# Position-bias bands for an attention kernel: laid out by the host, with the last bucket's value taken off on GpSimd, instead of built and spread on the chip

## The chip, the cores and the metric

The kernel runs on one core of a Trainium2 chip. A core has five engines with queues of their own: TensorE (PE; its weight loads are shown as PEld), VectorE (DVE), ScalarE (ACT), GpSimd (POOL) and SyncE (SP), which here only issues DMAs. Sixteen DMA engines move data between DRAM and the on-chip memory. The metric is the device time of one launch in microseconds; lower is better.

## The reference, cut to what matters

One layer of a decoder is computed for a prompt of 512 tokens and for 8 sample sequences of one new token each, which have 1024 past tokens in paged caches. Two mixers run side by side on the same modulated input: a sparse attention of 8 heads with three branches (compressed blocks, selected blocks, sliding window), and a block-sparse attention of another 8 heads (MoBA). Gates, projections and a layer norm follow. Every attention logit gets a bias that depends on the distance between query and key alone, through a table of 32 buckets by 16 heads:

```python
def t5_bucket(dist):
    n = jnp.maximum(dist, 0)
    nf = jnp.maximum(n, 1).astype(jnp.float32)
    large = MAX_EXACT + (jnp.log(nf / MAX_EXACT) / math.log(MAX_DISTANCE / MAX_EXACT)
                         * (N_BUCKETS - MAX_EXACT)).astype(jnp.int32)
    return jnp.where(n < MAX_EXACT, n, jnp.minimum(large, N_BUCKETS - 1))

s_w = jnp.einsum('bqgrd,bkgd->bqgrk', qc, kw) * scale + bias_w      # bias_w from tab[t5_bucket(distance)]
p_w = masked_softmax(s_w, valid_w)
```

From a distance of 128 (MAX_DISTANCE) on, all keys have the last bucket. A softmax doesn't change when one value is added to all its logits. So the kernel works with the bias less that of the last bucket: it is zero for every key that is far enough away, and only a band of 256 keys, those of the query's own block of 128 and the block before it, needs anything added.

## The kernel before, in words

All the work is matrix products on TensorE with float32 values split into a high and a low part (`hl`, `kd` and `q2`, `qx`): a product is three matmuls, and each weight tile is split by ScalarE (L310) and by VectorE or GpSimd (L231). The instructions are written as generators that are merged by their shares of the work (`merge`). From the program the tile framework makes one fixed order for each engine's queue, with semaphores; an engine runs its queue in order. A tile waits for its slot until the tile that had the memory before is no longer read.

The stages are: the adaLN modulation and the first projections (0 to about 50 us in the profile), the other projections with the compression (`phi`, to about 170 us), then eight steps `attend(pi)` of a pair of heads each, merged with the decode for the sample (`dec_a`, `dec_b`) and with further projections, and from about 500 us the gates, the up and output projections and the norm.

The bands go this way. `tables` (L458) multiplies the bucket table (`tabx`) by a matrix that holds, for 384 distances, which bucket is taken and the last one to subtract (L465), and copies the 16 by 384 result to the tile `bs`. Much later, in `phis` (L933), behind the last compression pair, GpSimd issues one DMA that writes each of the 16 rows 128 times to DRAM (`band_d`, L939), with rows 385 apart, 3 MB in all. In the attention, `prepare(pi)` (L956) loads for a pair of heads a tile of 128 x 2 x 256 (`bt`, tag `band`, two slots; L960), with a step of 384 between partitions, so that each query row finds its band shifted by one. `prepare(0)` is called before the first step, `prepare(pi + 1)` at the start of `attend(pi)`. `score` (L1000) adds the band to the logits of the last 256 keys on VectorE (L1011).

`prepare` also makes the split queries: `q2` by ScalarE and VectorE (L968, L969), `qx` by ScalarE and GpSimd (L970, L971). GpSimd also scales the exponentials (`p`, L1017).

SyncE's queue around the first band holds, in this order: a store of key/value rows (L572), the loads of the first two bands (L960), 64 loads of pages for the decode's selected keys (`raw<-slck`, L721), the window keys (L1134) and a bias table for them (`ew`, L1190 and L1191). At the start it holds small loads of constants (L540 to L547) behind those of the modulation weights.

Of the kernel before, what the change touches and what calls it, by code (L numbers as in the profile page):

```python
# [24 lines left out]
BIG = 1e30  # L25
# [26 lines left out]
NORM_N = 512  # L52
LIM_N = 384
PARTS = [512], [512], [512], [256, 256]
BAND_AT = 3
SELI_K = 6
W_FIRST = 3
COPY_ENG = "daa"
# [132 lines left out]
def build(tc, A):  # L191
# [44 lines left out]
    with ExitStack() as es:  # L236
# [25 lines left out]
        def p_e():  # L262
            return bank("e", 1)
# [109 lines left out]
        snew = per.tile([128, 3], F32, name="snew")  # L373
        dn = per.tile([128, 16], F32, name="dn")
        ocmp = per.tile([128, 128], F32, name="ocmp")
        m_d = dram.tile([8, 128, 2, NT], F32, name="m_d")
        band_d = dram.tile([16, 128, 385], F32, name="band_d")
        y = yp.tile([128, 8, NT], F32, name="y", tag="y")

        def const(name, rows=128):  # L380
# [77 lines left out]
        def tables():  # L458

            nc.gpsimd.memset(bc[:, :, 0:16], 0.0)  # L460
            nc.gpsimd.memset(bc[:, :, 31:64], BIG)
            nc.gpsimd.memset(cv2, 0.0)
            nc.gpsimd.memset(zn, 0.0)
            p = p_e()
            mm(p[:16, :384], tabx[:, 0:16], e[:, E_BAND:E_CMP], True, True)  # L465
            bs = st.tile([16, 384], F32, name="bs")
            nc.vector.tensor_copy(bs, p[:16, :384])
            D["band"] = bs
            p = p_e()
            for m in range(15):  # L470
                mm(p[:, m * 8:m * 8 + 8], e[:, E_CMP + m * 128:E_CMP + m * 128 + 128], tabx[:, 0:8], True, True)
            nc.vector.tensor_copy(bc[:, :, 16:31], p[:, :120].rearrange("p (m h) -> p h m", h=8))
            p = p_e()
            mm(p[:, :194], tabx[:, 16:144], e[:, E_DEC:E_WIN], True, True)
            mm(p[:, 256:386], tabx[:, 144:272], e[:, E_DEC:E_DEC + 130], True, True)
            nc.vector.tensor_copy(bdn, p[:, :194])
            nc.vector.tensor_copy(bdm, p[:, 256:386])
# [60 lines left out]
                    early_mm(n, j - 1)  # L538
        with tc.issue_after(ss["dma"].ins):
            nc.sync.dma_start(cstd, A["cst"][:, NC0:NC2])  # L540
            nc.sync.dma_start(pt16, A["pt16"])
            nc.vector.tensor_scalar(vidx, pt16, 16.0, const("p16"), op0=OP.mult, op1=OP.add)
            nc.sync.dma_start(phib, A["phib"])
            nc.sync.dma_start(pos, A["pos"].rearrange("p (a b c) -> p a b c", a=2, b=8))
            nc.sync.dma_start(ptt, A["pt"])
            nc.sync.dma_start(w2, A["w2"])
            nc.sync.dma_start(b2v, bass.AP(tensor=A["b2v"].tensor, offset=A["b2v"].offset, ap=[[0, 128], [1, 64]]))  # L547
# [385 lines left out]
        def phis():  # L933
            yield from phi_prompt(*kcvc)
            for bp in range(4):
                yield from phi_pair(bp)
                if bp == BAND_AT:
                    with tc.issue_after(D["last"].ins):
                        nc.gpsimd.dma_start(band_d[:, :, 0:384], D["band"].unsqueeze(1).to_broadcast([16, 128, 384]))  # L939

        merge(Flow(fills(FILLS[0]), fill_cost(FILLS[0])), Flow(phis(), PHIS))
        drain(dec_cmp())
# [13 lines left out]
        def prepare(pi):  # L956

            h0, hs = (pi, 4) if pi < 4 else (2 * pi, 1)
            bt = at.tile([128, 2, 256], F32, name="band", bufs=2)
            nc.sync.dma_start(bt, bass.AP(tensor=band_d.tensor, offset=band_d.offset + h0 * 128 * 385 + 127,  # L960
                                          ap=[[384, 128], [hs * 128 * 385, 2], [1, 256]]))
            BAND[pi] = bt
            for g in range(2):
                own, oth = OWN[g], OWN[1 - g]

                q2 = at.tile([128, T], F32R, name="q2", bufs=3)
                qx = at.tile([128, T], F32R, name="qx", bufs=3)
                nc.scalar.copy(q2[own], y[own, pi, :T])  # L968
                nc.vector.tensor_sub(q2[oth], y[own, pi, :T], f32(q2[own]))  # L969
                nc.scalar.copy(qx[oth], y[own, pi, :T])  # L970
                nc.gpsimd.tensor_sub(qx[own], y[own, pi, :T], f32(q2[own]))  # L971
                Q2[pi, g] = q2, qx
# [618 lines left out]
def _prepare(inp):  # L1591

    f = lambda a: np.ascontiguousarray(np.asarray(a))
    inp = {k: np.asarray(v) for k, v in inp.items()}
    cst, e = _constants()
    d = {"cst": cst, "e": e}
    call = np.concatenate([inp["c_prompt"], inp["c_sample"]], 0)
    d["cT"] = f(call.T.reshape(8, 128, 9).transpose(1, 0, 2))
    tab = np.concatenate([inp["rel_bias"], np.ones((1, 16), np.float32)], 0)
    tm = np.tile(tab[:, 8:].reshape(33, 4, 1, 2), (1, 1, 16, 1)).reshape(33, 128)  # L1600
    d["tabx"] = f(np.concatenate([tab, np.tile(tab[:, :8], (1, 16)), tm], 1))
    wa = inp["w_ada"][0]
    ws = np.concatenate([wa[:, 1024:2048].reshape(8, 128, 8, 128), wa[:, :1024].reshape(8, 128, 8, 128)], 3)
    d["ada_ss"] = f(ws.transpose(2, 1, 0, 3).reshape(8, 128, 2048))
    d["ada_g"] = f(wa[:, 2048:].reshape(4, 2, 128, 2, 512).transpose(3, 0, 2, 1, 4).reshape(8, 128, 1024))
    ba = inp["b_ada"][0]
    d["bT"] = f(ba[:2048].reshape(16, 128).T)
    d["rows"] = f(np.stack([ba[2048:], inp["ln_g"][0], inp["ln_b"][0]]))
    x = np.concatenate([inp["x_prompt"][0], inp["x_sample"][:, 0]], 0)
    d["xn"] = f(x)  # L1610
    d["xT"] = f(x.T.reshape(8, 128, NT))
    w = inp["w_in"][0]
    off = np.cumsum([0, 512, 128, 128, 128, 128, 128, 128, 24, 512, 512, 512, 512, 512, 1024, 1024])
    names = ["q", "kc", "vc", "ks", "vs", "kw", "vw", "ag", "z", "bq", "bk", "bv", "bz", "ma", "mb"]
    o = dict(zip(names, off))

    def cols(n):
        if n in o:
            return np.arange(o[n], o[n] + 128)
        base, k = n[:-1], int(n[-1])  # L1620
        if base in ("q", "z"):
            return np.concatenate([o[base] + (g * 4 + k) * 64 + np.arange(64) for g in range(2)])
        return o[base] + k * 128 + np.arange(128)

    wt = w.reshape(8, 128, -1)
    d["w_cols"] = f(np.stack([wt[:, :, cols(n)].transpose(1, 0, 2).reshape(128, 1024) for n in COLS]))
    d["w_ag"] = f(wt[:, :, o["ag"]:o["ag"] + 24].transpose(1, 0, 2).reshape(128, 192))
    w1 = inp["phi_w1"][0].reshape(2, 2, 8, 2, 64, 64)
    w1 = w1.transpose(0, 3, 4, 2, 1, 5)
    w1 = np.stack([w1[0], w1[1][:, :, :, ::-1]], 2)  # L1630
    d["w1"] = f(w1.reshape(128, 2 * 8 * 128))
    pos = inp["phi_pos"][0].reshape(2, 2, 8, 2, 64)
    d["pos"] = f(pos.transpose(3, 4, 0, 2, 1).reshape(128, 32))
    z = np.zeros((64, 128), np.float32)
    w2 = inp["phi_w2"][0]
    d["w2"] = f(np.concatenate([np.concatenate([np.tile(w2[0], (1, 2)), z], 0),
                                np.concatenate([z[:, :64], w2[1]], 0)], 1))
    d["phib"] = f(np.stack([inp["phi_b1"][0].reshape(128), np.tile(inp["phi_b2"][0, 0], 2)], 1))
    d["b2v"] = f(inp["phi_b2"][0, 1][None])
    cm = inp["cache_nsa_cmp"][:, 0].reshape(NPHYS, 8, 8, 2, 2, 2, 64)  # L1640
    d["cmp"] = f(cm.transpose(0, 3, 6, 4, 2, 5, 1).reshape(NPHYS, 128, 256))
    sl = inp["cache_nsa_slc"][:, 0]
    d["slck"] = f(sl[:, :, 0].transpose(0, 2, 3, 1).reshape(NPHYS, 128, 128))
    d["slcv"] = f(sl[:, :, 1].reshape(NPHYS * 16, 1024))
    mo = inp["cache_moba"][:, 0]
    d["mobk"] = f(mo[:, :, 0].reshape(NPHYS, 128, 4, 128).transpose(0, 3, 2, 1).reshape(NPHYS, 128, 512))
    d["mobv"] = f(mo[:, :, 1].reshape(NPHYS, 128, 512))
    wi = inp["state_nsa_win"][0].reshape(2, 4, 512, 2, 128)
    d["wink"] = f(wi[:, :, :, 0].transpose(0, 3, 1, 2).reshape(2, 128, 2048))
    d["winv"] = f(wi[:, :, :, 1].reshape(2, 4, 4, 128, 128).transpose(0, 3, 1, 2, 4).reshape(2, 128, 2048))  # L1650
    d["pt"] = f(inp["page_table"].reshape(1, NPAGE))
    d["pt16"] = f(np.repeat(inp["page_table"].T, 16, 0))
    ua = inp["w_up_a"][0].reshape(2, 4, 64, 1024).transpose(1, 0, 2, 3).reshape(4, 128, 8, 128)
    ub = inp["w_up_b"][0].reshape(4, 128, 8, 128)
    d["w_up"] = f(np.concatenate([ua, ub], 0).transpose(2, 1, 0, 3).reshape(8, 128, 1024))
    d["w_out"] = f(inp["w_out"][0].reshape(4, 2, 128, 2, 512).transpose(3, 0, 2, 1, 4).reshape(8, 128, 1024))
    return d
# [36 lines left out]
```

## Time and profile before

| what | us |
|---|---|
| median of 3 runs (lowest, highest) | 657.74 (655.98, 663.47) |
| the profiled execution's own time | 656.24 |
| its span, first to last instruction | 654.5 |
| TensorE busy | 610.4 |
| VectorE, ScalarE, GpSimd busy | 311.0, 294.9, 288.5 |
| mean granted clock of TensorE | 0.984 of full speed |

How to read the rows further down: times are microseconds from the span's start unless marked ns, L467 is line 467 of the kernel, `a<-b` is a tile and what it is computed or loaded from, `x16` a count. A busy TensorE isn't TensorE at its peak. "SPq" and "POOLq" are the queues' own instructions, DMA issues among them. Who ended a wait is inferred from semaphores.

### The profile page before, as it was taken

To read this page: it belongs to the slowest core of one execution; us is meant where nothing else is said; L and a number is where in the kernel's file an instruction comes from. 1 tells how busy PE (TensorE), PEld (TensorE's weight loads), DVE (VectorE), ACT (ScalarE), POOL (GpSimd) and SP (SyncE) were. 2 spreads that over 40 slices of the span, in tenths; PEclk is the share of its full clock that TensorE was granted. 3 is DMA by queue.
4 is the path that set the end of the run, shared out by engine and by line. 5 is a ranking of instruction groups with operands and counts; after the bars stand their busy time and mean duration, and the time that the engine had idled before them with its cause. 6 is when DMAs were issued, how large, how long until landed. Compare 5 with 4: busy or idle time off the path is not lost.

```text
span 654.5 us, 13320 instructions
## 1 busy us (share of the span) xinstructions
PE 610.4 (93%) x4747; PEld 509.7 (78%) x4747; DVE 311.0 (48%) x800; ACT 294.9 (45%) x679; POOL 288.5 (44%) x328
## 2 busy tenths in 40 slices
PE   5999999999979699999999899998987999999993
PEld 4779999999968378776879679866635998999672
DVE  1465545433563663334355447735431155545177
ACT  2247556434444445534445447635333353432521
POOL 1105586551442323433364545535332264655646
PEclk9999999999999979999999999999999999999997
DMA  8995565539943683798875562269887353345202
GB/s 305 355 292 187 169 193 171 170 76 109 200 140 103 203 334 109 251 312 290 262 252 157 209 226 91 62 224 325 295 265 280 97 166 126 97 130 180 78 28 104
DMA packets 64132, 124.77 MB, mean 191 GB/s; under 512 B 8142, under 2 KB 28368, under 8 KB 63521
## 3 DMA queue, kind: packets, MB, share of 16 engines
q1 hardware_dynamic: 61954, 116.58, 53.6%
q0 software_dynamic: 2112, 7.34, 6.3%
q8 instruction: 37, 0.61, 0.4%
q14 instruction: 29, 0.24, 0.1%
HBM read 112.76 MB, written 11.13 MB: 189 GB/s over the span
## 4 chain that ended last, share of the span: by engine, by line
PE 57%; DMA 12%; SPq 5%; DVE 3%; issue 2%; POOL 1%; ACT 1%; POOLq 0%; ACTq 0%; DVEq 0%
PE d L199 33%; PE s L199 8%; PE e L199 6%; DMA band_d<-bs 6%; SPq L721 4%; DMA raw<-mobv 4%; PE pt L1024 3%; PE o L202 2%; PE o L199 2%; PE pt L199 1%; PE e L202 1%; DMA ew<-tabx 1%; DMA raw<-slcv,vidx 1%; DMA raw<-winv 1%; SPq L717 1%
## 5 line engine op out<-in xcount | busy, mean ns | idle before, releaser
L199 PE MATMUL d<-hTh,hl 128*128 128x260 f32 (+1 forms) x1408 | 269.4, 288 | 1.6 <-DVE hl L231 1.1
L199 PEld LDWEIGHTS d<-hTh,hl 128*128 128x128 f32 (+1 forms) x1408 | 218.6, 187 | 15.8 <-issue 9.4
L199 PE MATMUL d<-hTl,hl 128*128 128x260 f32 (+1 forms) x704 | 199.5, 284 | 0.0
L199 PEld LDWEIGHTS d<-hTl,hl 128*128 128x128 f32 (+1 forms) x704 | 131.6, 187 | 3.1 <-issue 2.5
L231 POOL TENSOR_TENSOR hl<-raw,hl 128x512 fp32r<-128x512 f32 x56 | 74.0, 1321 | 101.6 <-ACT hl L310 97.0
L310 ACT CAST hl<-raw 128x512 fp32r<-128x512 f32 (+1 forms) x111 | 67.8, 615 | 75.5 <-PE d L199 63.0
L1017 POOL TENSOR_SCALAR p<-p,sm,gp 128x512 f32<-128x512 f32 (+1 forms) x64 | 39.9, 623 | 95.9 <-DVE sm L1016 91.3
L1015 ACT ACTIVATE p<-s,sm 128x512 f32<-128x512 f32 (+1 forms) x96 | 50.8, 529 | 66.9 <-PE pt L1024 52.2
L231 DVE TENSOR_TENSOR hl<-raw,hl 128x512 fp32r<-128x512 f32 (+1 forms) x55 | 53.5, 974 | 49.1 <-ACT hl L310 47.3
L199 PE MATMUL d<-yh,hl 128*128 128x260 f32 x256 | 46.3, 282 | 0.0
L1024 PE MATMUL pt<-cst,p 128*128 128x128 f32 x240 | 40.6, 283 | 1.5 <-DVE pp L1029 0.8
L199 PEld LDWEIGHTS d<-yh,hl 128*128 128x128 f32 x256 | 39.8, 188 | 1.0 <-issue 0.4
L199 PE MATMUL s<-kd,q 128*128 128x512 f32 (+1 forms) x96 | 35.2, 367 | 4.6 <-ACT p L1015 4.6
L1009 DVE TENSOR_REDUCE sm<-s 128x1 f32<-128x256 f32 (+1 forms) x48 | 16.9, 354 | 42.7 <-PE s L199 41.7
L1024 PEld LDWEIGHTS pt<-cst,p 128*128 128x128 f32 x240 | 28.0, 143 | 11.6 <-issue 5.9
L199 PE MATMUL d<-yl,hl 128*128 128x260 f32 x128 | 36.0, 282 | 0.0
L1017 POOL TENSOR_SCALAR p<-p,sm,cst 128x512 f32<-128x512 f32 (+3 forms) x32 | 19.5, 608 | 37.2 <-DVE sm L1016 36.8
L1011 DVE CUSTOM_DVE_ANT_0 s<-s,band 128x256 f32<-128x256 f32 (+1 forms) x48 | 17.3, 362 | 36.8 <-PE s L199 23.6
L199 PEld LDWEIGHTS s<-kd,q 128*128 128x128 f32 x96 | 18.4, 191 | 18.3 <-ACT p L1015 7.7
L199 PE MATMUL s<-u,w1h 128*128 128x256 f32 (+1 forms) x160 | 30.1, 283 | 2.1 <-ACT u L827 0.8
L199 PE MATMUL s<-kd,qx 128*128 128x512 f32 (+1 forms) x96 | 31.5, 331 | 0.0
L231 POOL TENSOR_TENSOR u<-craw,u 128x512 fp32r<-128x512 f32 x16 | 22.0, 1377 | 21.6 <-ACT u L827 21.6
(425 smaller groups left out, 1158.3 us busy)
## 6 DMA issues: line engine op xcount, KB each, us to landing
raw<-w_cols SPq DMA_DIRECT2D x46, 512.0 KB
raw<-mobk SPq DMA_DIRECT2D x64, 256.0 KB
raw<-mobv SPq DMA_DIRECT2D x64, 256.0 KB
u<-ada_ss SPq DMA_DIRECT2D x16, 512.0 KB
craw<-cmp SPq DMA_DIRECT2D x64, 128.0 KB
raw<-slck SPq DMA_DIRECT2D x64, 64.0 KB
raw<-ada_g SPq DMA_DIRECT2D x8, 512.0 KB
raw<-w_up SPq DMA_DIRECT2D x8, 512.0 KB
```

The costliest lines, as they stand in the source:

```text
L199: i = mmraw(out, lhsT, rhs, start=start, stop=stop, skip_group_check=True)
L202: i = mmraw(out, lhsT, rhs, start=start, stop=stop, skip_group_check=True)
L231: (nc.gpsimd if eng == "p" else nc.vector).tensor_sub(out, x, f32(hi))
L310: nc.scalar.copy(h, src)
L717: _, pages = nc.values_load_multi_w_load_instructions(ptt[0:1, k0:k0 + step * (len(outs) - 1) + 1:step], engines=(mybir.EngineType.SP,), m ...
L721: dyn.append(nc.sync.dma_start(out, A[name][bass.ds(page, 1)].rearrange("a p c -> p (a c)")))
L1009: nc.vector.tensor_reduce(sm[:, 0:1], s[:, :b], axis=AX, op=OP.min)
L1011: nc.vector.tensor_tensor_reduce(out=s[:, b:n], in0=s[:, b:n], in1=j.band[:, 256 - (n - b):], scale=1.0, scalar=top, op0=OP.add, op1=OP.mi ...
L1015: nc.scalar.activation(pr, s[:, :n], AF.Exp, scale=-1.0, bias=sm[:, 1:2], accum_out=sm[:, 2:3])
L1017: nc.gpsimd.tensor_scalar(pr, pr, sm[:, 3:4], j.gate(i), op0=OP.mult, op1=OP.mult)
L1024: nc.tensor.transpose(p[:, k * 128:k * 128 + 128], j.p[i][:, kb * 128:kb * 128 + 128], ident)
```

## The change

The host lays out the band of each pair of heads as 128 x 2 x 256 values, 2 KB for each partition, with the masked places at -1e30 and without the last bucket taken off. The table product, the tile `bs`, the 3 MB write and the DRAM tile go. Each `prepare` loads its band from this input. A new small tile `blast` holds the last bucket's value of the 16 heads on every partition; it is loaded in the row of small constants. Behind each band load GpSimd computes, for each of the two heads, (band - last) x -1 in place, 128 x 256 values.

```diff
-BAND_AT = 3
@@ build: tiles
+        blast = per.tile([128, 16], F32, name="blast")
         m_d = dram.tile([8, 128, 2, NT], F32, name="m_d")
-        band_d = dram.tile([16, 128, 385], F32, name="band_d")
@@ tables
-            p = p_e()
-            mm(p[:16, :384], tabx[:, 0:16], e[:, E_BAND:E_CMP], True, True)
-            bs = st.tile([16, 384], F32, name="bs")
-            nc.vector.tensor_copy(bs, p[:16, :384])
-            D["band"] = bs
@@ the row of small constants, behind the last load of modulation weights
             nc.sync.dma_start(cstd, A["cst"][:, NC0:NC2])
+
+            nc.sync.dma_start(blast, bass.AP(tensor=A["tabx"].tensor, offset=A["tabx"].offset + 31 * 272, ap=[[0, 128], [1, 16]]))
             nc.sync.dma_start(pt16, A["pt16"])
@@ phis
             for bp in range(4):
                 yield from phi_pair(bp)
-                if bp == BAND_AT:
-                    with tc.issue_after(D["last"].ins):
-                        nc.gpsimd.dma_start(band_d[:, :, 0:384], D["band"].unsqueeze(1).to_broadcast([16, 128, 384]))
@@ prepare
             bt = at.tile([128, 2, 256], F32, name="band", bufs=2)
-            nc.sync.dma_start(bt, bass.AP(tensor=band_d.tensor, offset=band_d.offset + h0 * 128 * 385 + 127,
-                                          ap=[[384, 128], [hs * 128 * 385, 2], [1, 256]]))
+            nc.sync.dma_start(bt, A["band"][pi])
+            for g in range(2):
+                h = h0 + g * hs
+                nc.gpsimd.tensor_scalar(bt[:, g], bt[:, g], blast[:, h:h + 1], -1.0, op0=OP.subtract, op1=OP.mult)
             BAND[pi] = bt
@@ _prepare, on the host
+    dist = 128 + np.arange(128)[:, None] - np.arange(256)[None]
+    heads = [[p, p + 4] if p < 4 else [2 * p, 2 * p + 1] for p in range(8)]
+    band = np.where((dist < 0)[..., None], np.float32(-BIG), inp["rel_bias"][_bucket(dist)])
+    d["band"] = f(np.stack([band[:, :, h].transpose(0, 2, 1) for h in heads]))
```

## Rows read from the trace of the kernel before

**Rows 1.** The page: the span, and each engine's busy time, share and instructions.

```profile
span 654.5 us, 13320 instructions
PE 610.4 (93%) x4747; PEld 509.7 (78%) x4747; DVE 311.0 (48%) x800; ACT 294.9 (45%) x679; POOL 288.5 (44%) x328
```

**Rows 2.** The chain that ended last, in order of time: start, length, what it was.

```profile
142.50 36.44 DMA band_d<-bs
179.00 0.38 SPq L960
...
210.01 1.79 DMA raw<-slck
...
221.86 5.21 DMA ew<-tabx
```

**Rows 3.** Who waited for whom over the span: us in total, times, longest.

```profile
SPq L960 <- DMA band_d<-bs: 9.2, 1, 9.2
SPq L960 <- DVE sm L1011: 13.8, 3, 7.2
POOL p L1017 <- DVE sm L1016: 128.1, 72, 5.4
```

**Rows 4.** SyncE's queue in order of time, around the first bands: start, length, what.

```profile
37.68 0.33 SPq L547 DMA_DIRECT2D b2v<-b2v  x1
...
166.72 3.01 SPq L572 DMA_DIRECT2D ok<-ev  x1
179.00 0.90 SPq L960 DMA_DIRECT2D band<-band_d  x2
180.43 40.45 SPq L721 DMA_DIRECT2D raw<-slck  x64
220.97 0.38 SPq L1134 DMA_DIRECT2D raw<-wink  x1
```

**Rows 5.** TensorE's waits from 180 to 240 us: total, times, longest.

```profile
PE e L199 <- DMA raw<-slck: 5.3, 4, 3.4
PE e L199 <- DMA ew<-tabx: 2.5, 1, 2.5
PE s L199 <- ACT p L1015: 2.1, 3, 1.3
PE d L199 <- DVE hl L231: 1.1, 1, 1.1
```

**Rows 6.** TensorE in order of time, two matmuls behind a wait (in brackets).

```profile
191.60 0.59 PE L199 MATMUL e<-raw,zn 128*32 128x512 f32 x1 [3.44 <-DMA raw<-slck]
...
227.21 1.83 PE L199 MATMUL e<-ew 33*128 33x512 f32 x2 [2.46 <-DMA ew<-tabx]
```

**Rows 7.** Stretches: length, busy PE PEld DVE ACT POOL, granted clock, DMA share, GB/s.

```profile
170.00:180.00 10.00, 9.82 (x80) 9.57 (x81) 7.76 (x16) 6.20 (x12) 6.51 (x8) 1.00 0.98 221
...
188.00:192.00 4.00, 0.56 (x6) 0.32 (x8) 1.94 (x9) 1.15 (x5) 2.87 (x3) 1.00 0.35 99
...
224.00:228.00 4.00, 1.54 (x8) 0.80 (x8) 3.23 (x5) 2.72 (x6) 2.03 (x1) 0.93 0.99 345
228.00:232.00 4.00, 4.00 (x13) 1.07 (x12) 1.34 (x3) 0.00 (x0) 0.55 (x1) 0.50 1.03 418
232.00:236.00 4.00, 3.67 (x18) 3.26 (x17) 2.27 (x7) 3.56 (x9) 1.72 (x2) 0.50 1.04 413
236.00:240.00 4.00, 4.00 (x30) 4.00 (x29) 3.17 (x9) 0.42 (x1) 0.80 (x1) 0.79 1.04 403
```

**Rows 8.** The table product at the start, and PEld's wait for its copy.

```profile
6.55 1.43 PE L199 MATMUL e<-y 33*16 33x384 f32 x2 [6.55 <-DMA y<-e]
...
PEld e L199 <- DVE bs L467: 0.8, 1, 0.8
```

**Rows 9.** GpSimd groups by shape: busy us, mean ns of one, idle before.

```profile
L1017 POOL TENSOR_SCALAR p<-p,sm,gp 128x256 f32<-128x256 f32 x16 | 8.9, 554 | 16.5 <-DVE sm L1016 14.1 <-PE d L199 2.2
L768 POOL TENSOR_SCALAR t<-t 128x256 f32<-128x256 f32 x4 | 2.2, 556 | 0.3
L1449 POOL TENSOR_SCALAR xs<-xs 128x256 f32<-128x256 f32 x1 | 1.0, 1014 | 0.3 <-POOL yl L231 0.3
```

**Rows 10.** GpSimd in order of time, and VectorE's two splits from 172 to 185.

```profile
173.43 1.28 POOL L231 TENSOR_TENSOR hl<-raw,hl 128x512 fp32r<-128x512 f32 x1 [3.16 <-ACT hl L310]
...
176.43 4.34 POOL L971 TENSOR_TENSOR qx<-y,q 64x512 fp32r<-64x512 f32 x3
...
L231 DVE TENSOR_TENSOR hl<-raw,hl x2: 684/1693/2702, 180.0 to 184.9; 128x512 fp32r<-128x512 f32 x2
```

## What the change does to the time, predicted

> **What bounds the kernel.** I read the views in this order: the page, the chain that ended last, SyncE's queue, TensorE's waits, then the other engines around the place these point to.
>
> The page says that TensorE is busy for 93% of the span [rows 1]. So a microsecond on another engine counts only where TensorE stands still for it, or where TensorE's own work shrinks. The chain that ended last shows such a place at once: its longest single piece is the write of the bands to DRAM, 36.44 us from 142.50 to 178.94 [rows 2]. What stands behind it is seen in SyncE's own waits and queue. SyncE comes to the load of the first band at 166.72 + 3.01 = 169.7 and waits 9.2 us there for the write [rows 3]. Its queue runs in order, and behind the band stand the 64 page loads of the decode's selected keys (`slck`), which take 40.45 / 64 = 0.63 us each to issue, then the window keys and `ew` [rows 4].
>
> TensorE pays for it between 180 and 240: four waits for `slck`, 5.3 us together, and one for `ew`, 2.5 us [rows 5]. The largest of the four is 3.44 us, before 191.60 [rows 6]. And the clock falls: granted 0.93 in 224 to 228, 0.50 in the next eight microseconds and 0.79 to 240 [rows 7], which is 1.2 GHz for most of that time. Against the full clock this is 4 x (0.07 + 0.50 + 0.50 + 0.21) = 5.1 us. Before it fell, TensorE was busy for 1.54 of 4.00 us, behind a stretch full of waits; one deep gap alone, 0.56 of 4.00 in 188 to 192, left the clock at 1.00 [rows 7].
>
> **The change, part by part.**
>
> *The write and the wait.* No band comes from the chip any more, so SyncE issues both bands at 169.7 and the `slck` loads from 170.6, about 9.2 us earlier. Sixteen loads make one tile, so a tile is issued every 10.1 us: the four are issued by about 181, 191, 201 and 211, and land 1.8 us later by the chain's row for the last wait [rows 2]. TensorE, held by nothing, would come to them at 188.2 (191.60 - 3.44 [rows 6]) and then, with each earlier wait taken off, between 4 and 5 us after each landing. All four waits go: **-5.3**. The load of `ew` was issued at 221.86 and took 5.21 us [rows 2]; 9.2 earlier it lands at 217.9, and TensorE comes to it at 227.21 - 2.46 - 5.3 = 219.4 [rows 6]. That wait goes too: **-2.5**.
>
> The row for the write is 36.44 us for 3 MB [rows 2]. The Trainium skill, page "DMA: Bandwidth & Descriptors", section "Anatomy of one DMA — SWDGE (gpsimd) path", fits such a transfer as 2.0 us plus its bytes over 436 GB/s, which I estimate at 9.2 us here: the write would be over at 152, before SyncE asks, and both terms above would be nil. The trace does not agree, the wait stands in it as a row of its own, so the rule gets no chance as a rival.
>
> *The clock.* It can give back between 0 and 5.1 us. In front of the fall TensorE's idle time is made of the last wait for `slck`, the one for `ew`, which both go, and short waits on ScalarE's exponentials, 2.1 us over three places [rows 5], which stay. As one gap alone left the clock up, I take a value near the upper end: **-4.0**.
>
> *The background.* The 3 MB are also off the DMA engines from 142 to 179. I cost that at nothing: TensorE was busy for 9.82 of 10.00 us even in the last ten of them [rows 7].
>
> *The start.* One table product and its copy go. It took TensorE 1.43 us from 6.55, and the next table product waited 0.8 us for the copy [rows 8]. Everything up to 6.55 is a wait for the table itself, which stays. The gain lies between 0 (the modulation weights still arrive when they arrive) and 2.2; I take **-1.0**. The load of `blast` adds one issue to SyncE's queue at about 33, at 0.33 us by the load of the same form behind it [rows 4]. It moves what follows by that much; the loads there run ahead of their use, so I cost it at nothing, and at 0.3 us if they don't.
>
> *The subtraction, first two pairs.* Each pair gets two TENSOR_SCALARs of 128x256 on GpSimd. The same operation with a per-partition scalar and two steps takes 0.554 us (16 of them); with constants 0.556; one in the tail took 1.014 [rows 9]. I take 0.55. Four of them, 2.2 us, fall into the stretch where GpSimd runs without a break from 173.43 to 182.7 and makes the `qx` tiles that the first scores need [rows 10]. Beside these, VectorE's split of a weight took 2.702 us instead of 0.684 [rows 10], so another 2.0 us can be lost there. The price lies between 0 (the bands land before 173.43, and GpSimd has just idled 3.16 us) and 4.2; as TensorE has weight matmuls in between, I take **+1.5**.
>
> *The subtraction, the six later pairs.* These are 12 x 0.55 = 6.6 us on an engine that is busy for 44% [rows 1] and mostly waits for VectorE [rows 3]; that by itself is hidden. New is a wait: GpSimd runs in order, and if it comes to a subtraction before the band has landed, the normalisations of `p` (L1017) and half of the weight splits (L231) stand behind it. A load is asked for a whole pair ahead of its use, so mostly it has landed. Price between 0 and the rival below; I take **+1.3**.
>
> Sum: -5.3 - 2.5 - 4.0 - 1.0 + 1.5 + 1.3 = **-10.0 us**. The span of 654.5 becomes 644.5 and the profiled execution's 656.24 becomes 646.2. The median of the runs shown, 657.74, stands 1.5 above that execution, so I forecast **647.7**.
>
> **The rivals.**
>
> *A: the gap is passed on.* The waits for DMA go, but GpSimd and VectorE, both crowded from 173 to 184, take their place: the two `qx` and the splits come late by the full 4.2 us, the stretch keeps its holes, and the clock falls as before. For it: the 2.702 us of the row above, and a wait of TensorE for that very split, 1.1 us [rows 5]. Against it: TensorE has other matmuls to run there. Time: 657.7 - 5.3 - 2.5 - 1.0 + 4.2 + 1.3 = 654.4. The Trainium skill, page "SBUF — State Buffer", section "Who interferes with whom", says that a VectorE instruction with two SBUF inputs and a GpSimd instruction that reads SBUF exclude each other for their whole length. By that rule 16 subtractions can hold VectorE for up to 8.9 us in all; the trace agrees as far as the long split goes.
>
> *B: the wait isn't the band's.* SyncE may be held at 169.7 by something else that ends little before 179, such as the memory of the new tiles, which lies over that of the start and of the compression. Then the waits stay, and only the start and the subtraction count: 657.7 - 1.0 + 2.8 = 659.5. Against it: SyncE's wait is put down to the write, and the write's end at 178.94 fits the issue at 179.00 [rows 2, 4].
>
> *C: slower, GpSimd stands for the later bands.* SyncE itself waits up to 7.2 us for a band's slot [rows 3], so the load may be issued late, while GpSimd already stands at the subtraction. A small load in a crowded stretch took 5.21 us from issue to landing [rows 2]. Six pairs at that price, with nothing in hand, are 31.3 us: 657.7 - 11.3 + 31.3 = 677.7. From 11.3 / 6 = 1.9 us of TensorE per pair it eats the gain; from 3.0 us per pair the kernel is more than 1% slower. Against it: the pair in between lasts tens of microseconds.
>
> **The numbers.** Chances: forecast 0.55, A 0.25, B 0.10, C 0.10. The forecast alone reaches from 657.7 - 17.2 = 640.5 (every gain at its upper bound, 5.3 + 2.5 + 5.1 + 2.2, the exponentials' 2.1 too, and no cost) to about 651, where the clock gives nothing back and the rest holds. The range for 8 in 10 goes from 641 to 657, over most of A, and leaves out B and C. A difference under 1%, 6.6 us, can hardly be told from none here. Faster by more than that: the forecast and the best of A, 0.58. Within 1%: the rest of A and B, 0.32. Slower: C, 0.10.
>
> **What would show it.** Right: no wait of SyncE at the band load, the first `slck` load at about 170, no TensorE wait for `slck` or `ew`, a granted clock of 1.00 from 180 to 240. Wrong in the last steps: TensorE or ScalarE waiting for GpSimd's L231 or `qx`, or GpSimd idle in front of the subtraction, released by a band's DMA. Wrong as a whole: the first `slck` load still near 179. The forecast also fails if the instructions of an engine come out in another order, since the program is ordered anew.

## The result, and the profile after

The changed kernel takes 662.47 us (median of 22 runs, 657.36 to 667.57), the kernel before 657.39 us (22 runs, 654.47 to 663.47) on the same chips. The ratio is 1.0071 with a 95% interval of 1.005 to 1.0091: slower by about 4.7 us, where 647.7 us, faster by 10, was forecast. The range of 641 to 657 does not hold it. Ratios here and below leave out executions more than 1.5% above the fastest of their kernel, so a ratio can differ from that of the two medians. The profiled execution took 662.21 us with a span of 660.5.

Where the forecast looked, it was right. SyncE's queue around the first band, after (start, duration, queue and line, operation, count); it answers to [rows 4]:

```profile
171.03 0.35 SPq L568 DMA_DIRECT2D ok<-ev  x1
171.49 0.87 SPq L953 DMA_DIRECT2D band<-band  x2
173.12 40.61 SPq L717 DMA_DIRECT2D raw<-slck  x64
213.83 0.38 SPq L1129 DMA_DIRECT2D raw<-wink  x1
...
214.72 0.30 SPq L1186 DMA_DIRECT2D ew<-tabx  x1
```

SyncE no longer stands at the band, and the page loads begin at 173.12 instead of 180.43. So the microseconds were won, and lost elsewhere. To see where, I cut both executions at the same places of the program: the store ahead of the first band, and the first, third, fourth and eighth time that ScalarE puts out a finished pair of heads (`y<-o`, L1052 before, L1047 after). Windows of before, from the start to that store, then to the first, third, fourth and eighth output, then to the end (length; busy time and count of TensorE, its weight loads, VectorE, ScalarE, GpSimd; granted clock; DMA share; GB/s):

```profile
0.00:166.72 166.72, 157.52 (x1286) 144.85 (x1287) 74.06 (x164) 78.58 (x166) 69.24 (x81) 1.00 0.70 202
166.72:251.01 84.29, 73.08 (x515) 58.45 (x514) 49.07 (x136) 39.44 (x99) 31.55 (x39) 0.94 0.65 195
251.01:368.81 117.80, 117.80 (x966) 94.00 (x967) 49.47 (x169) 53.91 (x140) 50.16 (x58) 1.00 0.72 240
368.81:414.02 45.21, 42.11 (x399) 34.95 (x399) 29.57 (x89) 27.45 (x72) 22.34 (x28) 0.96 0.46 146
414.02:497.23 83.21, 75.39 (x569) 50.28 (x573) 35.17 (x119) 38.06 (x103) 32.68 (x43) 1.00 0.75 255
497.23:654.50 157.27, 144.54 (x1022) 127.18 (x1014) 73.66 (x124) 57.42 (x104) 82.53 (x81) 0.98 0.36 118
```

The same windows of after:

```profile
0.00:171.03 171.03, 159.63 (x1290) 146.22 (x1290) 77.22 (x166) 78.78 (x167) 65.89 (x81) 1.00 0.59 193
171.03:244.30 73.27, 69.58 (x518) 57.21 (x519) 48.98 (x136) 40.63 (x100) 37.82 (x44) 0.98 0.58 193
244.30:366.08 121.78, 119.61 (x987) 94.92 (x987) 50.16 (x168) 53.72 (x139) 56.06 (x64) 0.99 0.71 237
366.08:416.92 50.84, 41.70 (x366) 34.49 (x366) 28.09 (x88) 27.10 (x69) 23.38 (x28) 0.93 0.36 119
416.92:503.37 86.45, 77.55 (x573) 50.62 (x573) 34.78 (x119) 38.05 (x102) 38.12 (x46) 0.98 0.75 254
503.37:660.50 157.13, 144.31 (x1014) 127.33 (x1014) 73.96 (x124) 57.32 (x103) 81.15 (x80) 0.98 0.34 113
```

By stretch, after less before: +4.3, -11.0, +4.0, +5.6, +3.2, -0.1, together +6.0. The stretch of the bands won 11.0. The start and the three stretches from the first to the eighth output lost 17.2, most of it as idle time of TensorE (length less busy time): 9.2 to 11.4 at the start, 0 to 2.2, 3.1 to 9.1 and 7.8 to 8.9 behind. Some of the rest is the clock: granted 0.99, 0.93 and 0.98 in the three stretches behind, 1.00, 0.96 and 1.00 before.

Two places in the trace of after, at the start and at the third pair. TensorE's waits from 40 to 60 us (who waits, for whom, us in all, times, longest), then from its timeline and GpSimd's the third pair (start, duration, what, idle time before it and its end):

```profile
PE d L198 <- DVE hTh L451: 2.7, 1, 2.7
```

```profile
331.48 0.95 POOL L1134 DMA_INDIRECT raw<-slcv,vidx  x1 [0.30 <-issue]
337.11 1.26 POOL L966 TENSOR_TENSOR qx<-y,q 64x512 fp32r<-64x512 f32 x1 [4.68 <-DMA raw<-slcv,vidx]
```

```profile
338.98 0.66 PE L1019 MATMUL pt<-cst,p 128*128 128x128 f32 x4 [2.10 <-POOL p L1012]
```

Before has no wait there for `hTh`, the high part of the modulated input. And there GpSimd made this `qx` ahead of its `slcv` loads; after, it stands behind them (loads of the selected keys' values) for 4.68 us, the `p` behind it comes late, and TensorE stands for 2.10. So instructions stand in another order. That can be counted in the two built programs, without a time: compared engine by engine, with line and buffer numbers taken off, TensorE's queues differ from the row behind the table product on, and 1850 of its 2585 rows stand in another place. The first rows of before, then of after:

```
L199 MATMUL e<-y 16x384          (the table product)
L199 MATMUL s<-u,cs 32x256 x4
L199 MATMUL e<-y 128x8 x10
L199 MATMUL s<-u,cs 32x256 x4

L198 MATMUL e<-y 128x8 x12
L198 MATMUL s<-u,cs 32x256 x4
L198 MATMUL e<-y 128x8
L198 MATMUL s<-u,cs 32x256 x4
```

The theories to tell apart: (1) the order in which the queues were dealt anew is the loss; (2) the 16 subtractions on GpSimd are; (3) whatever comes early at the bands is lost at 350 to 500 again, in any order.

### The profile page after: what moved, and what is told of

Its sections match the earlier page's. It is cut to its first block, busy times and chain, and to the rows that moved or that the text cites. A ratio compares the mean times of both kernels' runs of the same rounds, so it can differ in the third digit from the quotient of the medians.

```text
span 660.5 us, 13339 instructions
## 1 busy us (share of the span) xinstructions
PE 612.4 (93%) x4745; PEld 510.8 (77%) x4745; DVE 313.2 (47%) x799; ACT 295.6 (45%) x679; POOL 302.4 (46%) x343
## 4 chain that ended last, share of the span: by engine, by line
PE 75%; DMA 8%; DVE 8%; ACT 3%; issue 3%; SPq 2%; POOL 1%; POOLq 0%; ACTq 0%; DVEq 0%
PE d L198 44%; PE s L198 12%; PE e L198 7%; DMA raw<-mobv 3%; PE pt L1019 3%; PE o L198 2%; PE pt L198 2%; PE o L201 2%; DMA raw<-slcv,vidx 2%; SPq L717 1%; DMA raw<-winv 1%; PE e L201 1%; DVE q L964 1%; DVE hl L230 1%; DMA y<-e 1%
## 5 line engine op out<-in xcount | busy, mean ns | idle before, releaser
L230 POOL TENSOR_TENSOR hl<-raw,hl 128x512 fp32r<-128x512 f32 x56 | 72.6, 1297 | 101.1 <-ACT hl L309 95.4
L230 DVE TENSOR_TENSOR hl<-raw,hl 128x512 fp32r<-128x512 f32 (+1 forms) x55 | 50.1, 910 | 61.0 <-ACT hl L309 54.7
L966 POOL TENSOR_TENSOR qx<-y,q 64x512 fp32r<-64x512 f32 x16 | 24.3, 1520 | 23.5 <-ACT q L963 18.7
L1004 DVE TENSOR_REDUCE sm<-s 128x1 f32<-128x256 f32 (+1 forms) x48 | 17.1, 355 | 36.5 <-PE s L198 35.7
```

Of the source, the lines that this page charges most:

```text
L230: (nc.gpsimd if eng == "p" else nc.vector).tensor_sub(out, x, f32(hi))
L1004: nc.vector.tensor_reduce(sm[:, 0:1], s[:, :b], axis=AX, op=OP.min)
```

## The experiments

"Rows elsewhere" counts TensorE's rows that stand in another place than in the kernel before (of about 2585). As it goes by place, a moved row can shift those behind it into the count; it says which kernels keep the order rather than how much of it moved. Ratios are against runs of the kernel before on the same chip.

| run | rows elsewhere | median, us | ratio to before (95%) |
|---|---|---|---|
| tab_kept | 1652 | 655.88 | 0.9973 (0.9942, 1.0005) |
| nosub | 1764 | 659.92 | 1.0023 (0.9987, 1.0059) |
| early_write | 1447 | 675.70 | 1.0267 (1.0217, 1.0317) |
| mult_add | 1651 | 660.86 | 1.0049 (1.0020, 1.0079) |
| order_kept | 0 | 655.61 | 0.9998 (0.9962, 1.0035) |
| before_sub | 1184 | 666.49 | 1.0169 (1.0119, 1.0219) |
| no_write | 1341 | 653.44 | 0.9943 (0.9901, 0.9985) |
| sub_on_vectore | 2 | 654.43 | 0.9974 (0.9933, 1.0015) |
| thin_write | 0 | 644.68 | 0.9785 (0.9742, 0.9829) |
| thin_vectore | 2 | 648.09 | 0.9856 (0.9807, 0.9905) |
| thin_mult_add | 125 | 645.29 | 0.9775 (0.9714, 0.9837) |
| two_columns | 1821 | 660.14 | 1.0031 (0.9996, 1.0065) |
| thin_no_product | 1456 | 654.15 | 0.9938 (0.9904, 0.9972) |
| thin_subtract | 1184 | 654.68 | 0.9978 (0.9938, 1.0017) |

### One part undone at a time

**tab_kept**: the changed kernel, with the five lines of the table product and its copy (L464 to L468 of before) back in `tables`.

> The changed kernel with the old table product (1.43 us on TensorE) and its copy by VectorE put back at the start, where nothing reads them any more; all instructions of the program up to the point where the old kernel issued its write then stand in the old order on TensorE, VectorE, ScalarE. Theory 1, the new program's other order costs the start about 4.3 us: the last store ahead of the band loads is issued at 166.7 to 167.5 us instead of 171.03, although work was added, TensorE is again 5.00 busy in 50 to 55, and the end comes at 656 if nothing behind it changes; behind it the order differs from both kernels, so 650 to 662. Theory 2, the subtraction on GpSimd is the whole loss: the store stays near 171 or later (work was added), and the time is within 2 us of the changed kernel.

The store is issued at 166.56, TensorE is busy for 5.00 of 5.00 in 50 to 55, the ratio is 0.9973 instead of 1.0071: work was added, and 1% of the time went. That speaks for theory 1. (The profiled execution took 661.05 us.)

**nosub**: the changed kernel without

```diff
-            for g in range(2):
-                h = h0 + g * hs
-                nc.gpsimd.tensor_scalar(bt[:, g], bt[:, g], blast[:, h:h + 1], -1.0, op0=OP.subtract, op1=OP.mult)
```

> The changed kernel without its 16 subtractions on GpSimd: the bands are added as the host laid them out, neither lessened by the last bucket's value nor negated, so the scores are others (this part of the computation is left out); every other instruction is there. Theory 2, the 18.6 us of GpSimd in front of the softmax products are the loss behind 245 us: the end falls by 10 to 16 us, to 645 to 651, and GpSimd's share falls by 18.6 us. Theory 1, the loss is the order in which the queues were dealt: the start stays at about 171.0 for the last store ahead of the bands, the first pairs gain the 5.05 us at 175.56 at most, and the end is 653 to 664.

659.92 us: some 3 us go with the subtractions, by the intervals of the two ratios at most about 6; theory 2 asked for 645 to 651. TensorE's idle time from the third to the fourth output is still 8.4 us.

**early_write**: the kernel before with

```diff
-BAND_AT = 3
+BAND_AT = 2
```

> The kernel before, its 3 MB write issued one cmp pair earlier (behind the third pair instead of the fourth), nothing removed or added: if the write takes 36.4 us as before it lands at about 150 to 165, ahead of the band load's place in SyncE's queue (169.8). The start up to there is dealt as before. Theory 1 (the wait of 9.2 us was worth some 10 us at 180 to 245, and what comes behind is dealt anew by chance): SyncE does not wait at the band, no TensorE wait for slck or ew over 1 us, the first output of a pair at 241 to 246 instead of 251.0, the end at 641 to 658. Theory 2 (subtraction is the whole loss): all of the 9 us is kept to the end, 644 to 648. If the write in its earlier place slows the chunk loads beside it, the start is longer by up to 3 us.

Neither theory's time: 675.70 us, and the start is longer by 17 us where up to 3 were allowed. GpSimd issues the write at 123.95, and it takes 35.7 us. SyncE's queue, then TensorE's waits from 100 to 190:

```profile
129.66 14.67 SPq L721 DMA_DIRECT2D craw<-cmp  x4
149.15 33.47 SPq L342 DMA_DIRECT2D raw<-w_cols  x5
```

```profile
PE d L199 <- ACT hl L310: 13.4, 1, 13.4
```

Four page loads whose issue otherwise takes 1.88 us take 14.67, and the weights behind them come late. The write holds up other loads that SyncE issues while it runs, not only the one that waits for its data.

**mult_add**: the changed kernel with

```diff
-blast[:, h:h + 1], -1.0, op0=OP.subtract, op1=OP.mult)
+-1.0, blast[:, h:h + 1], op0=OP.mult, op1=OP.add)
```

> The changed kernel with each subtraction written as band times -1.0 plus the value of the last bucket (multiply by a constant, then add a column) instead of subtract a column, then multiply by -1.0. If the operation is what makes it 1.14 us, the 16 take 0.45 to 0.56 us each as the other two-step products of 128x256 do, 8.0 us in all instead of 18.6. If the form of the operands (a column and a constant) makes it, they stay at 1.13 to 1.14 us. Theory 2: the end gains 6 to 9 us with it, to 652 to 655. Theory 1: the order is dealt anew or the gain is lost, 655 to 664.

The operation takes 0.484 us in the median instead of 1.140, so the operation and not the form of its operands makes the price; the time, 660.86, is theory 1's.

### The order held still

Which rows move can be seen in a built program before anything runs. Reading the band from the host's table, and nothing else, moves none.

**order_kept**: the kernel before with

```diff
-            nc.sync.dma_start(bt, bass.AP(tensor=band_d.tensor, ...
+            nc.sync.dma_start(bt, A["band"][pi])
```

> The kernel before with one line changed: the band load reads the table laid out by the host instead of band_d. Table product and 3 MB write are still made, and nothing reads what is written; no subtraction or negation, so the bands added to the scores are others (this part of the computation is left out). Every instruction of TensorE, VectorE, ScalarE and GpSimd then stands in the order of the kernel before, only SyncE's wait at the band load is gone. Theory 1 (the gain is real and was lost to the other order): the band loads are issued at 169.5 to 171 instead of 179.0, no idle time of TensorE over 1 us for slck or ew, first pair's output at 241 to 244 instead of 251.0, and all of it stays to the end: 645 to 650. Theory 3 (whatever lets the pairs come earlier lays open the chain of slcv and winv loads at 350 to 420, whatever the order): the idle time of TensorE from the third to the fourth pair's output rises from 3.1 to 6 us or more, and the end is 652 to 658.

Theory 1 misses, and theory 3 has the time but not its reason. Nothing is lost behind the bands (3.25 us idle from the third to the fourth output, 3.10 before), but next to nothing is won at them. SyncE's queue and the DMA engines' share in the last windows of the write (columns as above):

```profile
165.53 3.13 SPq L572 DMA_DIRECT2D ok<-ev  x1
168.76 6.81 SPq L960 DMA_DIRECT2D band<-band  x2
176.69 41.78 SPq L721 DMA_DIRECT2D raw<-slck  x64
```

```profile
170.00:180.00 10.00, 10.00 (x83) 9.91 (x84) 7.77 (x14) 6.08 (x12) 7.39 (x9) 1.00 1.00 250
```

Free of the semaphore, the issue of two band loads takes 6.81 us, since the DMA engines are full of the write until about 178. That gives theory 4: the write itself must go as well, and the order must stay.

**before_sub**: the kernel before with a subtraction that changes nothing behind each band load.

```diff
+            for g in range(2):
+                nc.gpsimd.tensor_scalar(bt[:, g], bt[:, g], zc0, 1.0, op0=OP.subtract, op1=OP.mult)
```

> The kernel before, each band slice passed once more through GpSimd (a column of zeros taken off, times 1.0: the same operation as the subtraction, and the same result as without). It adds the 16 operations alone: the wait for the write, the write and the table product stay, the start is in the old order, but behind the first band load the queues come in another order (1184 of 2585 rows of TensorE). Theory 2 (the subtraction is the loss): slower by 8 to 13 us, 665 to 671, with TensorE waiting for GpSimd's p. Theory 1 (the other order is the loss): the change has no cost of its own above 5 us, and what it does shows at 300 to 420 as idle time behind slcv, winv and ScalarE's p, not for GpSimd: 657 to 666.

666.49 us, 1.7% slower, is the time that theory 2 gave and lies just outside theory 1's. The trace, of an execution of 661.87 us, shows more of theory 1's signs: from 244 to 505 TensorE waits 6.8 us for ScalarE's `p` (3.2 before), 1.5 for `slcv` (0.2 before) and 1.2 for GpSimd's `p` (none before). Operation and order came together here, so this run doesn't part them.

**no_write**: order_kept without the `BAND_AT` write. **sub_on_vectore**: order_kept with blast loaded and `nc.vector.tensor_scalar(... op0=OP.subtract, op1=OP.mult)` in `prepare`.

> As the kernel whose band load reads the host's table with table product and no subtraction (the bands added to the scores are others), but the 3 MB write is taken out as well. The start keeps the old order, behind the write's place the queues come in another order (1341 of 2585 rows of TensorE), with no subtraction in the program. Theory 1: the gain at the bands is there (load issued at 166 to 170, first pair's output 242 to 247), but part or all of it is lost at 300 to 510 in idle time of TensorE: 649 to 658, and 3 us or more above the kernel in which the write is kept and the order is the old one. Theory 2: no loss without the subtraction, within 2 us of that one, or faster.

> Host's bands with the subtraction and negation on VectorE instead of GpSimd, blast loaded, table product and the 3 MB write kept though nothing reads them. All but 2 rows of TensorE, 2 of GpSimd and 14 of VectorE (the subtractions themselves) stand in the order of the kernel before. Theory 1: it keeps the gain at the bands, less what the subtraction costs on VectorE (16 of 128x256, an estimate of 0.3 to 0.5 us each from VectorE's 128x256 operations, the first four ahead of the first scores): 646 to 653. Theory 3: 652 to 658. Theory 2 says nothing here beyond that GpSimd is free of it: 646 to 650.

653.44 and 654.43 us. The first has neither wait, write nor subtraction and gains only 0.6%: 1341 rows stand elsewhere. That it would stand above order_kept was a miss, since that one had not won anything. The second has the old order but the write; it misses theory 1's 646 to 653 and has theory 3's time, for the reason that order_kept showed: its two band loads take 7.00 us to issue.

### Old order and no write

The order turned out to hang on the number of pieces of the write, not on their size: with 128 rows of 8 columns in place of 384 no row of TensorE moves, with 64 rows of 384 there are 1240.

**thin_write**: order_kept with

```diff
-  nc.gpsimd.dma_start(band_d[:, :, 0:384], D["band"].unsqueeze(1).to_broadcast([16, 128, 384]))
+  nc.gpsimd.dma_start(band_d[:, :, 0:8], D["band"][:, 0:8].unsqueeze(1).to_broadcast([16, 128, 8]))
```

**thin_vectore** is sub_on_vectore with the same edit; **thin_mult_add** has mult_add's operation on GpSimd instead.

> As the kernel that only reads the host's table and keeps the old order (bands added to the scores are others, no subtraction), with the write into band_d cut to the first 8 of 384 columns: still 2048 pieces, but 64 KB in place of 3 MB, and nothing reads it. All rows of TensorE, VectorE, ScalarE and GpSimd stand in the order of the kernel before. Theory 4 (new: without its wait the band load stood 6.81 us behind the write in the DMA queues, so the write has to go as well; and the gain holds if the order behind it is kept): the two band loads are issued within 1 us at 166 to 169, slck is issued at 167 to 170 instead of 176.7, the first pair's output comes at 240 to 244 and the eighth at 487 to 492, the end at 643 to 649. Theory 3 (what comes early at the bands is lost at 350 to 500 in any order, to the chain of slcv, winv and mobv loads): first output 240 to 244, eighth 493 to 498, end 650 to 656. If 2048 small pieces take as long as large ones, nothing changes: 651 to 656.

> The whole computation: host's bands, blast loaded, subtraction and negation on VectorE, table product kept, and the write cut to 64 KB, in the order of the kernel before but for 2 rows of TensorE. Theory 4: the thin write's time plus 0 to 3 us for the subtractions on VectorE, 644 to 651, faster than both kernels by 1 to 2%. Theory 3: 651 to 656.

> The whole computation: host's bands, blast loaded, times -1.0 plus blast on GpSimd (0.95 us each), table product kept, the write cut to 64 KB; 125 of 2585 rows of TensorE stand elsewhere than in the kernel before. Theory 4: 645 to 651. Theory 3: 651 to 657. Against the thin write without subtraction it shows what the 15.2 us of GpSimd work cost when the order is nearly the same: an estimate of 1 to 4 us from the first four ahead of the first scores.

644.68, 648.09 and 645.29 us: theory 4's time in all three, and theory 3 falls. One sign missed: in the profiled execution of thin_write (648.66 us) the start took until 171.43 (granted clock 0.96, 1.00 in before), so the band loads came at 171.88 and `slck` at 173.72. (The 0.95 us quoted there was misread: it is a row of two operations.) The last two compute everything the layer needs, and both beat the kernel before and the changed one. SyncE's queue of thin_mult_add, then its windows at the same six places:

```profile
165.76 0.35 SPq L574 DMA_DIRECT2D ok<-ev  x1
166.22 0.90 SPq L962 DMA_DIRECT2D band<-band  x2
168.26 40.36 SPq L723 DMA_DIRECT2D raw<-slck  x64
```

```profile
0.00:165.76 165.76, 157.20 (x1286) 144.72 (x1287) 75.93 (x164) 78.91 (x167) 69.17 (x81) 1.00 0.60 198
165.76:236.13 70.37, 67.50 (x515) 55.19 (x514) 49.17 (x136) 39.13 (x99) 35.19 (x45) 1.00 0.61 203
236.13:354.75 118.62, 117.89 (x966) 94.12 (x967) 49.52 (x169) 53.72 (x140) 51.92 (x62) 1.00 0.71 238
354.75:400.22 45.47, 41.98 (x399) 34.76 (x399) 29.64 (x89) 27.44 (x71) 24.53 (x30) 0.96 0.44 146
400.22:483.13 82.91, 74.92 (x569) 50.29 (x573) 34.85 (x119) 37.97 (x102) 35.76 (x45) 1.00 0.75 257
483.13:639.90 156.77, 144.72 (x1022) 127.12 (x1020) 73.49 (x124) 57.47 (x104) 82.33 (x81) 0.98 0.35 117
```

The stretch of the bands takes 70.37 us instead of 84.29, and every other one is within 1 us of before, with TensorE's counts the same. What was won stays to the end.

What the moved rows cost shows best at the fourth pair. TensorE's waits from the third to the fourth output, after (366.08 to 416.92):

```profile
PE s L198 <- ACT p L1010: 4.5, 4, 2.2
PE e L198 <- DMA raw<-winv: 1.9, 1, 1.9
PE e L198 <- DMA raw<-slcv,vidx: 1.8, 1, 1.8
```

thin_mult_add (354.75 to 400.22):

```profile
PE s L199 <- ACT p L1019: 2.0, 3, 1.4
PE e L199 <- DMA raw<-slcv,vidx: 0.6, 1, 0.6
PE e L199 <- DMA raw<-winv: 0.6, 1, 0.6
```

The waits are for the same tiles, and longer. In this stretch TensorE is idle for 2.9 to 3.8 us in the six kernels of the old order (before, order_kept, sub_on_vectore, thin_write, thin_vectore, thin_mult_add), and for 4.7 to 9.1 us in the ten of other orders. It also has less to run there: 399 matmuls in each of the six, 342 to 367 in the ten. In after, 28 of the 33 that are missing run in the three stretches ahead (1290, 518 and 987 instead of 1286, 515 and 966). That the waits come out longer because fewer matmuls are left to fill them fits this, but no run tests it.

### What each part costs by its order

**two_columns**: the changed kernel with a column of -1.0 for the constant; **thin_no_product**: thin_mult_add with the product replaced by `nc.vector.memset(bs, 0.0)`; **thin_subtract**: thin_mult_add with the changed kernel's operation.

> The changed kernel with the constant -1.0 of the subtraction in a column of SBUF, so that both operands are columns as in the softmax products of 128x256 (0.55 us): subtract a column, times a column. If the mixture of a column and a constant makes the operation slow (1.14 us here, 0.95 us as multiply by a constant plus a column), they take 0.5 to 0.6 us; if subtracting or adding makes it slow, 0.95 to 1.15 us. Time: within 4 us of the changed kernel, 658 to 664; 134 of 2584 rows of TensorE stand elsewhere.

> As the whole computation with host's bands, times -1.0 plus blast on GpSimd, and the write cut to 64 KB, but without the table product: its 16 rows of 384 are set to zero by VectorE instead, and nothing reads them. Up to the write the queues stand in the order of the changed kernel (TensorE's first 654 rows), behind it in a third order. If the product's removal itself gains (the prediction's step, 1.0 us, 0 to 2.2): within 2 us of the kernel that keeps it (645.3), or faster. If the start's new order costs time: 648 to 655, with the last store ahead of the bands 2 to 5 us later, and part of it at 180 to 500.

> As the whole computation with host's bands on GpSimd and the write cut to 64 KB, the product kept, but subtracting first and then times -1.0, as the changed kernel does (1.14 us each instead of 0.61). TensorE stands in the old order to row 855, behind it 1184 of 2585 rows stand elsewhere: the same order as in the kernel before with the operation added. If the slow operation and the order that it brings cost what they cost there (11 us): 653 to 659. If only the operations themselves count (16 times 0.5 us, the first four ahead of the first scores): 646 to 650.

The operation by itself, in after, two_columns and thin_mult_add on GpSimd (shortest, median, longest in ns, first and last start):

```profile
L956 POOL TENSOR_SCALAR band<-band,blast x16: 1133/1140/1482, 175.6 to 454.0; 128x256 f32<-128x256 f32 x16
```

```profile
L958 POOL TENSOR_SCALAR band<-band,blast,neg x16: 1209/1221/1723, 175.6 to 451.5; 128x256 f32<-128x256 f32 x16
```

```profile
L965 POOL TENSOR_SCALAR band<-band,blast x16: 475/480/1181, 177.8 to 437.3; 128x256 f32<-128x256 f32 x16
```

So the form with a subtraction is slow (with two columns even a little above the range expected), not the mixture of a column and a constant. Against thin_mult_add's 0.9775, the product's removal costs 1.6% of the time before (0.9938) and the slow operation with its order 2.0% (0.9978), some 10.7 and 13.3 us of 657; taking the write out altogether costs 1.6% against thin_write (0.9943 to 0.9785). The intervals of the ratios of each such pair don't meet. In the slower kernel of each 1184 to 1456 rows stand elsewhere. Two of the three edits take work away and add at most one memset, so it is what is dealt anew with them that costs the time. The changed kernel makes all three edits and stands 3.0% above thin_mult_add, so they don't add up.

The product's removal can be followed in thin_no_product. Its windows from the start to the store, to the first output, and from the third to the fourth:

```profile
0.00:169.78 169.78, 158.25 (x1284) 145.30 (x1285) 76.73 (x164) 78.91 (x167) 67.28 (x81) 1.00 0.59 193
169.78:244.40 74.62, 69.31 (x518) 56.09 (x517) 47.95 (x141) 40.32 (x101) 35.27 (x45) 0.98 0.58 192
363.11:411.69 48.58, 41.43 (x367) 34.59 (x367) 28.75 (x89) 27.37 (x71) 21.25 (x28) 0.93 0.35 115
```

Against thin_mult_add these are 4.0, 4.3 and 3.1 us longer, of 11.3 in all between the two profiled executions.

What stays open: in thin_subtract and before_sub the longer operation and the order that it brings aren't parted, so theory 2 falls as the whole loss, but not as a share of it. Nor is it shown why the old order is the better one; that its lists and shares were fitted to it is only a guess, and a new fit for the changed kernel wasn't tried. Single executions differ: with the same start order the store ahead of the bands was issued between 165.06 and 171.43, with the changed kernel's between 167.92 and 171.05, so the 4.3 us of the start in the one profile above are partly chance. The idle time of TensorE ahead of that store is not: 11.0 to 12.1 us in the five kernels without the product, 7.9 to 9.2 in the ten with it (early_write apart).

## Why the prediction was wrong, step by step

*The wait, slck and ew: right.* -7.8 forecast. In thin_mult_add, with the order held, the idle time of the bands' stretch falls from 11.21 to 2.87, -8.3, and no wait for `slck` or `ew` is left. In the changed kernel itself it falls to 3.69, with 0.7 us of waits for `slck`.

*The clock: right, and slightly above the upper end.* -4.0 forecast, of at most 5.1. The same 515 matmuls take 67.50 us instead of 73.08, -5.6, with the granted clock at 1.00 instead of 0.94, that is 2.4 GHz throughout. In after it is only partly given back: TensorE was busy for 7.14 of 10.00 us in 180 to 190 and 0.85 was granted in the next ten (windows as above):

```profile
180.00:190.00 10.00, 7.14 (x51) 5.28 (x50) 8.15 (x23) 3.86 (x11) 6.42 (x8) 0.98 0.35 99
190.00:200.00 10.00, 10.00 (x71) 10.00 (x72) 5.07 (x15) 5.38 (x13) 3.43 (x5) 0.85 0.38 106
```

*The background: wrong, but without a share in the sum.* "I cost that at nothing." order_kept and early_write show that the write itself holds up the loads that SyncE issues behind it: without the semaphore, `slck` came only 3.7 us earlier (176.69). The sign stood in [rows 4]: the store at 166.72 took 3.01 us to issue, 0.35 after. I put the whole 9.2 us down to the semaphore. The estimate of 9.2 us by the fit of the Trainium skill, page "DMA: Bandwidth & Descriptors", section "Anatomy of one DMA — SWDGE (gpsimd) path", fails here a second time: issued elsewhere, the write took 35.7 us.

*The start: wrong in sign.* -1.0 forecast, 0 to -2.2. The product's 1.43 us went, and the modulation's instructions were dealt anew around the hole: TensorE waits 2.7 us for `hTh` at 50 to 55 (2.6 in thin_no_product, none in before), and thin_no_product takes 1.6% of the time before more than the kernel with the product, in the profiled executions about a third of it at the start.

*The subtraction: its size wrong, its place right.* 0.55 us was called the price of "the same operation", but [rows 9] shows products, and a multiply with an add, and no subtraction; that takes 1.14, so the first four took 5.05 us instead of 2.2. As a multiply and an add they took 2.68 in thin_mult_add, and all 16 cost nothing that can be measured (0.9775 with them, 0.9785 without). Rival C falls: after, GpSimd waited for a band's load 3.4 us in all, in three places.

*Rival A: a small part of it came true.* In after, VectorE's subtraction on `c` took 3.61 us at 181.90 beside GpSimd's splits, 0.42 before, and TensorE stood 1.9 us for the tile made of it. VectorE's operation, then the second of GpSimd's splits:

```profile
181.90 3.61 DVE L1064 TENSOR_TENSOR c<-c,cst 128x256 f32<-128x256 f32 x1
183.97 1.25 POOL L230 TENSOR_TENSOR hl<-raw,hl 128x512 fp32r<-128x512 f32 x1
```

VectorE's operation reads two tiles and ends at 185.51, just behind the split's end at 185.22. That agrees with the Trainium skill, page "SBUF — State Buffer", section "Who interferes with whom": a VectorE instruction with two SBUF inputs contends with a GpSimd instruction that reads SBUF. Rival B falls: SyncE issued the band load at once. Something like it was true of the kernel before, where the wait's end alone would have freed little (order_kept). The measured time lies between B's and C's, but by a mechanism that no rival had.

*The step that failed* is the frame of the sum: every term was read from a row of before and taken to stand in the same queue order, and the prediction's last sentence, that the forecast fails if "the instructions of an engine come out in another order", stood there without a chance or a price. The runs showed in its place that the order is a term as large as the gain: the product's removal, forecast at -1.0 us, cost 10.7 with the order that it brought, and the slow subtraction, forecast at +2.8, cost 13.3 with its own. The changed kernel stands 3.0%, some 19 us, above thin_mult_add, where nearly the old order is kept.

With the order held the forecast of 647.7 is met by 645.29 (GpSimd) and 648.09 (VectorE), but partly by luck. In thin_mult_add the stretch of the bands gave 13.9 us where wait and clock were forecast at 11.8; the 2.8 for the subtraction were not paid there; and the 1.0 at the start could not be won, since both kernels keep the product. By the ratios the two gained 14.8 and 9.5 us of 657.7, 10 being forecast. (The forecast's upper end without the clock's gain is 651.7 by its own sum, not about 651.)

## What to carry to other kernels

Where a framework deals the queues, compare the order of the built programs before costing an edit: removing 1.4 us of work put about half of TensorE's rows in another place here and cost 1.6%. Test a gain in two steps, first with the old order held by a harmless stand-in (here a DMA with as many pieces but 64 KB), then with the work really gone. And when a load waits for a transfer, ask what the transfer does to the loads that don't.

## What the runs showed of the hardware that was not expected

- A two-step operation of 128 x 256 float32 values on GpSimd takes 1.14 us in the median when a subtraction is followed by a multiply, with a column and a constant (1.140) or two columns (1.221), and 0.48 us as a multiply and an add (0.63 on average in thin_mult_add, single ones up to 1.18). VectorE did the subtracting form in 0.391 us on average in sub_on_vectore.
- A write of 3 MB in 2048 pieces from 16 partitions takes 36.4 us in the kernel before, with the DMA engines at a share of 0.97 to 1.01 from 150 to 179. In early_write, issues of page loads on SyncE stretch beside it from 0.47 to 3.7 us each (1.88 and 14.67 us for four). With pieces of 32 bytes instead of 1536, 2048 pieces land in 5.9 to 6.6 us (five runs).
